# Ten of sixteen input tiles of the out-projection's second half as seven-product blocks, in the stream that later runs the up-projection

## The chip, the core and the metric

One core of one Trainium2 chip runs the whole program. The metric is the device time in microseconds (us) of one execution. The median of three executions of the kernel before is 2817.67 us (2817.4 to 2818.12); the profiled execution took 2819.0 us, of which its trace covers a span of 2816.9 us.

TensorE (PE) multiplies, VectorE (DVE), ScalarE (ACT) and GpSimd (POOL) do elementwise work, and SyncE (SP) issues most DMA transfers. Each engine works through its own instructions in order and waits on semaphores.

## The reference, cut to what matters

One layer of a hybrid decoder on 544 tokens (512 of a prompt, 32 of eight samples), all in fp32:

```python
proj = rmsnorm(x, norm_mix_w) @ w_in              # 2048 -> 9248 columns
y    = rmsnorm(ssd(...) * silu(z), ssd_norm_w)    # 2048 channels, "SSD half"
u    = cf_a * sigmoid(cf_g)                       # 2048 channels, "conv half"
u    = silu(layernorm(causal_dwconv(u, 31 taps)))
x    = x + concat([y, u]) @ w_out                 # out-projection, 4096 -> 2048
h    = rmsnorm(x, norm_ffn_w)
g, v = split(causal_dwconv(h @ w_up, 3 taps))     # 2048 -> 2 x 5504
x    = x + (silu(g) * v) @ w_down
out  = rmsnorm(x, norm_final_w)
```

The states of the three convolutions and of the SSD are outputs too.

## The kernel before

Channels stand on partitions in tiles of 128, and the 544 tokens stand in the free dimension as two halves of 272. A matrix product takes one 128x128 piece of weights and one half of the tokens. Each fp32 operand is split into a rounded part h and a remainder l (both fp32r), and three products are summed: h*xh, h*xl and l*xh. So a pair of weight tile and input tile costs 3 matmuls per half, 6 in all.

The work runs in two machines, one after the other.

**Jobs** (`job`, `run_jobs`, lines 137 to 219). A job makes one output tile of 128 channels from 16 input tiles in four blocks of four. `pump` keeps up to five weight blocks loaded (`raw`, 128x512) and three or four split (`wh` on ACT, line 118; `wl` on POOL or DVE, line 119). `tick` runs between blocks: it issues what `delay` and `store` put off, and one step of the generators in `bg`. Jobs in order: the first three columns of the input projection run together ("dt"), then the rest of it, then the out-projection's SSD half ("oy", 16 jobs, each times the norm factor `ry`, plus the residual `xT` on POOL, stored to DRAM as `xr_dram`), then its conv half ("ou", 16 jobs, evacuated by adding to the tile read back from `xr_dram`). While "oy" runs, `ln_gen` normalizes the 16 conv tiles `U` and splits each into `Uh` and `Ul`.

**Items** (lines 1194 to 1285, loop at 1558). One stream of products, prepared two items ahead: `prep_h` (ACT cast, line 1254), `prep_l` (DVE, line 1263), `product` on PE, `evac` of the item before. A `Group` of seven items computes two output tiles from K pairs of input tiles by Strassen's scheme: the 2x2 blocks are two output tiles by (first K, second K input tiles) by two token halves. Seven block products replace eight, at 3*K matmuls each. Its weights come in five tiles; two of those are sums of two pieces, which are made by a plain load from SP followed by an accumulating DMA from POOL (line 1231); one more sum is made on DVE (`sum_a`, `sum_b`). The inputs' sums `T` are made by `prep_pair` (lines 1128 to 1152). A `Plain` item computes one output tile from K input tiles, 6*K matmuls. The stream holds 43 groups with K = 8 (up-projection, `xs` times `w_up`) and then the down-projection, mixed of `Plain` items and groups with K = 6. Five weight buffers (`wr`) rotate; `issue` starts the next load when a split or sum has read one.

The `T` pairs for the up-projection are made in the evacuations of "ou", the last two around the switch from jobs to items. The norm factor `r2` is computed there too (`rsqrt_gen`, matmuls with `ones`, line 239).

At the start, `start_step` (line 307) makes `xh` on ACT and `xl` on DVE for four input tiles at a time, and `squares` (line 338) makes the squares for the first norm, two of four on ACT and two on DVE, and adds them up. `dt_gen` computes the SSD step sizes; PE needs its `dA_tok` in the matmul at line 422.

Of the kernel before, what the change touches and what calls it, by code (L numbers as in the profile page):

```python
# [14 lines left out]
NT = 544  # L15
NH = 272
# [7 lines left out]
NS0 = 4  # L24
# [6 lines left out]
def hymba_step_kernel(ctx: ExitStack, tc: tile.TileContext, a: dict):  # L31
# [236 lines left out]
    with tc.manual_schedule():  # L268
# [69 lines left out]
        def squares(n):  # L338
            def f():
                for k in range(4 * n, 4 * n + 4):  # L340
                    x = xraw.pop(k)
                    sq = slot("sq") if k > 1 else acc[k]
                    if k % 4 < 2:
                        S.activation(sq, x, AF.Square)
                    else:
                        V.tensor_tensor(sq, x, x, ALU.mult)
                    if k > 1:
                        e, i = (G, 0) if k % 4 == 0 else (V, 1)
                        e.tensor_tensor(acc[i], acc[i], sq, ALU.add)
            return f  # L350
# [23 lines left out]
        def dt_gen():  # L374
# [626 lines left out]

        xr_dram = [dram.tile([128, NT], F32, name=f"xrd{t}") for t in range(16)]
        xre = {}
        Uh, Ul = {}, {}

        def ln_gen():
# [34 lines left out]
            def fin(t):  # L1041
                u = U_t.pop(t)

                def f1():
                    Uh[t] = slot("Uh", dt=F32R, side=t < NS0)
                    S.copy(Uh[t], u)

                def f2():
                    Ul[t] = slot("Ul", dt=F32R, side=t < NS0)
                    V.tensor_tensor(Ul[t], u, Uh[t].bitcast(F32), ALU.subtract)  # L1050
                V.tensor_tensor(u, u, R["rs"], ALU.mult)
                S.activation(u, u, AF.Silu, scale=cfw[:, t, 32:33], bias=cfw[:, t, 33:34])
                delay(1, f1)
                delay(2, f2)
            for t in list(range(U_SPILL, 16)) + list(range(NS0, U_SPILL)) + list(range(NS0)):
                if t == 0:
                    Cur.side = swap("side0", "side1", bufs=2 * NS0, side="right")
                fin(t)
                yield
            yield  # L1060
            yield
# [4 lines left out]
        def load_x(t):  # L1066
            xre[t] = slot("xre")
            Y.dma_start(out=flat(xre[t]), in_=a["xT"][t])

        def oy_pre(t):  # L1070
            def f():
                if t == 0:
                    bg.append(ln_gen())
                    load_x(0)
                if t + 1 < 16:
                    load_x(t + 1)
            return f

        def oy_evac(t):
            def go(ps):  # L1080
# [5 lines left out]
                def s1():  # L1086
                    G.tensor_tensor(o, o, xre.pop(t), ALU.add)

                def s2():
                    store(xr_dram[t], flat(o))  # L1090
                return [s0, s1, s2]
            return go

        for t in range(16):
            job("oy", out_srcs(t, 0), lambda k: (Yh[k], Yl[k]), oy_evac(t), G, oy_pre(t))

        xres, xs, T_t = {}, {}, {}
        fst = dict(acc=None)
        xr2_dram = [dram.tile([128, NT], F32, name=f"xs{t}") for t in range(16)]
        OT = [t for k in range(8) for t in (k, k + 8)]  # L1100

        def load_xr(i):
            t = OT[i]
            xres[t] = slot("xres")
            Y.dma_start(out=flat(xres[t]), in_=xr_dram[t])

        def ou_pre(i):
            def f():
                if i == 0:
                    while not idle():  # L1110
                        tick()
                    load_xr(0)
                if i + 1 < 16:
                    load_xr(i + 1)
                else:
                    delay(0, up_open)
                    for j, f in enumerate(x_pair(6)):
                        delay(j // 2, f)
            return f
# [34 lines left out]
        def x_pair(k):  # L1154
            return prep_pair(T_t, k, lambda: xs[k], lambda: xs[k + 8])

        NPRE = 6

        def ou_evac(i):
            t = OT[i]  # L1160

            def go(ps):
                x = xres.pop(t)
                sq = slot("sq")

                def s0():
                    V.tensor_tensor(x, mv(ps), x, ALU.add)
                    xs[t] = slot("xs")
                    S.activation(xs[t], x, AF.Copy, scale=nw[:, NW_FFN, t:t + 1])
                    store(xr2_dram[t], flat(x))  # L1170

                def s1():
                    S.activation(sq, x, AF.Square)
                    if fst["acc"] is None:
                        fst["acc"] = sq
                    elif i < 15:
                        G.tensor_tensor(fst["acc"], fst["acc"], sq, ALU.add)
                    else:
                        spawn(rsqrt_gen([fst["acc"], sq], setr("r2")), 3)
                steps = [s0, s1] if i < 15 else [lambda: None, s0, s1]  # L1180
                if i % 2 and i // 2 < NPRE:
                    steps += x_pair(i // 2)
                return steps
            return go

        for i in range(16):
# [504 lines left out]
```

## Time and profile before

| | |
|---|---|
| median of three executions | 2817.67 us |
| profiled execution, its span | 2819.0 us, 2816.9 us |
| PE busy | 2780.4 us of the span |
| DVE, ACT, POOL busy | 2089.3, 1211.1, 905.1 us |
| "ou" jobs | 1198.0 to 1391.8 us of the span |
| up-projection | 1392.9 to 2313 us |
| down-projection and last norm | 2314 to 2817 us |

PE is busy almost all the time, and the idle time sits in a few places: the first 50 us, the switch from jobs to items, and the last norm. The other engines have room on average. The DMA share of a stretch is the mean busy share of the core's 16 DMA engines.

### The profile page before, as it was taken

The page shows a single profiled execution, that of the slowest core. Times are in us where ns is not written, and L with a number is a line of the kernel's source. Part 1 is how long each engine was busy: PE and PEld are TensorE (multiplying, and loading weights), DVE is VectorE, ACT ScalarE, POOL GpSimd, SP SyncE. Part 2 cuts the span into 40 slices and gives each one's busy share as a digit, 9 for nine tenths or more (in the row PEclk, how much of TensorE's full clock was granted, in tenths as well). Part 3 has the DMA queues.
Part 4 walks back from the last instruction along what each step waited for, and adds up shares of the span by engine and source line. Part 5 has one row for each costly group of instructions (what it writes and reads, how often), then busy time and mean ns, then how long its engine had stood idle before and what let it go on. Part 6 is the DMA issues. An engine that isn't in the chain of part 4 may idle for free.

```text
span 2816.9 us, 55473 instructions
## 1 busy us (share of the span) xinstructions
PE 2780.4 (99%) x22214; PEld 2753.4 (98%) x22214; DVE 2089.3 (74%) x3180; ACT 1211.1 (43%) x1793; POOL 905.1 (32%) x922
## 2 busy tenths in 40 slices
PE   7999999999999999999999999999999999999998
PEld 7999999999999999999999999999999999999997
DVE  7576665677777778344498888888888887778775
ACT  4555444333333324334344444444444444344344
POOL 4476668666676765511100000000000000100103
PEclk9999999999999999999999999999999999999999
DMA  4233343333332354444467777777777776765761
GB/s 166 82 116 115 95 144 103 124 108 104 101 101 92 97 161 126 138 133 133 146 177 195 191 186 195 190 185 193 194 185 191 194 200 193 179 185 154 174 186 64
DMA packets 194371, 422.29 MB, mean 150 GB/s; under 512 B 38080, under 2 KB 42816, under 8 KB 194112
## 3 DMA queue, kind: packets, MB, share of 16 engines
q1 hardware_dynamic: 177120, 361.07, 41.2%
q0 software_dynamic: 16992, 57.68, 11.6%
q8 instruction: 174, 2.85, 0.4%
q14 instruction: 85, 0.70, 0.1%
HBM read 376.25 MB, written 42.41 MB: 149 GB/s over the span
## 4 chain that ended last, share of the span: by engine, by line
PE 95%; DVE 3%; DMA 1%; issue 1%; ACT 0%; SPq 0%; DVEq 0%; POOLq 0%; ACTq 0%
PE mm L229 43%; PE st L1281 13%; PE st L1279 13%; PE st L1280 13%; PE st L229 6%; PE ax L229 2%; DMA x<-in_xT 1%; DVE o L501 1%; PE ax L660 1%; PE ax L599 0%; DVE sl L1263 0%; PE ax L664 0%; PE ax L629 0%; PE ax L757 0%; PE ax L763 0%
## 5 line engine op out<-in xcount | busy, mean ns | idle before, releaser
L1281 PE MATMUL st<-Th,sl 128*128 128x272 f32 x2640 | 762.7, 289 | 2.6 <-DVE sl L1263 2.6
L1279 PE MATMUL st<-Th,sh 128*128 128x272 f32 x2640 | 762.3, 289 | 1.4 <-ACT sh L1254 1.4
L1280 PE MATMUL st<-Tl,sh 128*128 128x272 f32 x2640 | 761.7, 289 | 0.0
L119 POOL TENSOR_TENSOR wl<-raw,wh 128x512 fp32r<-128x512 f32 x336 | 448.9, 1339 | 408.0 <-ACT wh L118 360.5
L1254 ACT CAST sh<-wr 128x1024 fp32r<-128x1024 f32 (+3 forms) x343 | 327.1, 954 | 416.8 <-PE st L1280 334.9
L1281 PEld LDWEIGHTS st<-Th,sl 128*128 128x128 f32 x2640 | 496.8, 188 | 3.9 <-DVE sl L1263 3.9
L1279 PEld LDWEIGHTS st<-Th,sh 128*128 128x128 f32 x2640 | 496.9, 188 | 1.7 <-ACT sh L1254 1.6
L1280 PEld LDWEIGHTS st<-Tl,sh 128*128 128x128 f32 x2640 | 496.8, 188 | 0.0
L229 PE MATMUL mm<-xh,wh 128*128 128x272 f32 x2304 | 483.4, 291 | 7.4 <-ACT xh L313 7.4
L229 PE MATMUL mm<-xl,wh 128*128 128x272 f32 x2304 | 479.4, 289 | 4.8 <-DVE xl L315 4.8
L118 ACT CAST wh<-raw 128x512 fp32r<-128x512 f32 x416 | 255.4, 616 | 525.3 <-PE mm L229 415.6
L229 PE MATMUL mm<-xh,wl 128*128 128x272 f32 x2304 | 478.5, 289 | 0.0
L1263 DVE TENSOR_TENSOR sl<-wr,sh 128x1024 fp32r<-128x1024 f32 (+3 forms) x343 | 377.9, 1102 | 58.7 <-ACT sh L1254 58.6
L229 PEld LDWEIGHTS mm<-xh,wh 128*128 128x128 f32 x2304 | 368.1, 188 | 16.3 <-ACT xh L313 7.4
L229 PEld LDWEIGHTS mm<-xl,wh 128*128 128x128 f32 x2304 | 365.4, 188 | 6.2 <-DVE xl L315 6.2
L229 PEld LDWEIGHTS mm<-xh,wl 128*128 128x128 f32 x2304 | 365.2, 188 | 0.0
L1231 POOL DMA_DIRECT2D wr<-in_w_up x86 | 74.9, 871 | 829.5 <-DVE ws L1245 235.4
L942 DVE SCALAR_TENSOR_TENSOR ax<-w,cfw,ax 128x512 f32<-128x512 f32 x448 | 302.5, 746 | 7.1 <-ACT ax L918 6.8
L1254 ACT CAST sh<-ws 128x1024 fp32r<-128x1024 f32 (+1 forms) x118 | 117.1, 992 | 264.1 <-DVE ws L1241 147.0
L1263 DVE TENSOR_TENSOR sl<-ws,sh 128x1024 fp32r<-128x1024 f32 (+1 forms) x118 | 136.0, 1153 | 30.6 <-ACT sh L1254 21.1
L1231 POOL DMA_DIRECT2D wr<-in_w_down x32 | 27.9, 871 | 368.6 <-DVE pd L1405 141.6
L119 DVE TENSOR_TENSOR wl<-raw,wh 128x512 fp32r<-128x512 f32 x80 | 70.2, 883 | 94.6 <-ACT wh L118 94.6
(317 smaller groups left out, 4979.0 us busy)
## 6 DMA issues: line engine op xcount, KB each, us to landing
wr<-in_w_up SPq DMA_DIRECT2D x215, 512.0 KB, 4.8
raw<-in_w_in SPq DMA_DIRECT2D x292, 256.0 KB, 3.2
wr<-in_w_up POOLq DMA_DIRECT2D x86, 512.0 KB, 8.0
wr<-in_w_down SPq DMA_DIRECT2D x96, 384.0 KB, 3.5
raw<-in_w_out SPq DMA_DIRECT2D x128, 256.0 KB, 3.0
wr<-in_w_down POOLq DMA_DIRECT2D x32, 384.0 KB, 5.5
ad<-ra SPq DMA_DIRECT2D x43, 272.0 KB, 7.9
ar<-ad SPq DMA_DIRECT2D x43, 272.0 KB, 4.0
```

The costliest lines, as they stand in the source:

```text
L118: S.copy(h[:, :n], r[:, :n])
L119: (cur["wl"] or eng).tensor_tensor(l[:, :n], r[:, :n], h[:, :n].bitcast(F32), ALU.subtract)
L229: T.matmul(o, lhsT=w[:, c], rhs=x[:, hf, :], start=first, stop=last)
L501: V.scalar_tensor_tensor(o[:, 0:568], w[:, i:i + 568], scw[:, t, i:i + 1], o[:, 0:568], ALU.mult, ALU.add)
L660: T.matmul(yps[ro:ro + 64, c4[c]], lhsT=xdt[c][:, q, :], rhs=MT[:, c4[c]], start=True, stop=c == 0)
L942: V.scalar_tensor_tensor(p, w[:, i:i + 512], wt(i), p, ALU.mult, ALU.add)
L1231: G.dma_start(out=t, in_=more, accum_op=ALU.add)
L1254: S.copy(h, src)
L1263: V.tensor_tensor(l, src, h.bitcast(F32), ALU.subtract)
L1279: T.matmul(outs[0], lhsT=h[:, c], rhs=xh_, start=k == 0, stop=False)
L1280: T.matmul(outs[0], lhsT=h[:, c], rhs=xl_, start=False, stop=False)
L1281: T.matmul(outs[0], lhsT=l[:, c], rhs=xh_, start=False, stop=k == o.K - 1)
```

## The change

Of the conv half's 16 input tiles, ten (tiles 6 to 15) become five pairs, whose products go through `Group`s with K = 5, one group for each pair of output tiles, eight groups. The other six tiles (0 to 5) go through 16 `Plain` items with K = 6. These 56 + 16 items stand at the head of the stream; the "ou" jobs are gone, and the stream's weight buffers open in the last "oy" job. `ln_gen` makes the sums `T_u` of the five pairs and stores the six other tiles to DRAM (`un_dram`), from where they are read back and split while the groups run. "oy" no longer adds the residual: it stores the scaled product alone. For each output tile the stream loads `xT` into `xres` and lets POOL add `xr_dram` by an accumulating DMA. `prep_pair` for the up-projection runs as tasks beside the `Plain` items, the last pair in the first up item. In the very first item the products with `l` come last. The evacuation of the groups (`block_evac`) is the one that the down-projection had. The squares at the start are all made on ACT. `dt_gen` gets one more `yield`.

```diff
@@ squares
-                    if k % 4 < 2:
-                        S.activation(sq, x, AF.Square)
-                    else:
-                        V.tensor_tensor(sq, x, x, ALU.mult)
+                    S.activation(sq, x, AF.Square)
@@ ln_gen, after the norm factor
+            for t in range(UP):
                 fin(t)
+                store(un_dram[t], flat(U_t.pop(t)))
                 yield
+            for i in range(NU):
+                p, q = UP + i, UP + NU + i
+                fin(p)
+                fin(q)
+                yield
+                f = prep_pair(T_u, i, lambda: U_t[p], lambda: U_t[q])
...
+        def load_xr(t):
+            xres[t] = slot("xres")
+            Y.dma_start(out=flat(xres[t]), in_=a["xT"][t])
+
+        def add_xr(t):
+            G.dma_start(out=flat(xres[t]), in_=xr_dram[t], accum_op=ALU.add)
...
@@ oy_pre, t == 15
+                    while not idle():
+                        tick()
+                    load_xr(0)
+                    load_xr(8)
+                    delay(0, up_open)
+                    delay(2, lambda: add_xr(0))
+                    delay(3, lambda: add_xr(8))
@@ oy_evac
-                def s1():
-                    G.tensor_tensor(o, o, xre.pop(t), ALU.add)
...
-        for i in range(16):
-            job("ou", out_srcs(OT[i], 1), lambda k: (Uh[k], Ul[k]), ou_evac(i), V, ou_pre(i))
@@ product
-                T.matmul(outs[0], lhsT=l[:, c], rhs=xh_, start=False, stop=k == o.K - 1)
+                if q:
+                    T.matmul(outs[0], lhsT=l[:, c], rhs=xh_, start=False, stop=k == o.K - 1)
+            for k in range(0 if q else o.K):
+                T.matmul(outs[0], lhsT=l[:, k * 128:k * 128 + 128], rhs=o.T[m, k][0], start=False, stop=k == o.K - 1)
@@ before the up-projection's groups
+        for i in range(8):
+            lo, hi = (wout[t, :, 2048 + UP * 128:4096] for t in (i, i + 8))
+            q = len(items)
+            Group(lo, hi, NU, T_u, block_evac(i))
+            if i:
+                at_item(q - 5, lambda i=i: load_xr(i))
+                at_item(q - 2, lambda i=i: add_xr(i))
+                at_item(q - 2, lambda i=i: load_xr(i + 8))
+                at_item(q + 1, lambda i=i: add_xr(i + 8))
+        for t in range(UP):
+            at_item(28 + 4 * t, lambda t=t: u_load(t))
+            at_item(30 + 4 * t, lambda t=t: u_split(t))
...
+        for i in range(16):
+            Plain(wout[OT[i], :, 2048:2048 + UP * 128], UP, lambda k: (Uh[k], Ul[k]), out_evac(i))
+        for k in range(8):
+            st = prep_pair(T_t, k, lambda k=k: xs[k], lambda k=k: xs[k + 8])
+            for f, d in zip(st, (2, 2, 3, 3)):
+                at_item(q + 2 * k + d, f)
```

How the instructions move, in the built programs. First the start, DVE, kernel before (`xl` is a remainder of the input, `sq` a square, `acc` a sum of squares):

```order
L315 SCALAR_TENSOR_TENSOR xl_242<-x_88,nw,xh_240 128x544
L346 TENSOR_TENSOR sq_281<-x_86 128x544
L349 TENSOR_TENSOR acc_148<-acc_148,sq_281 128x544
L346 TENSOR_TENSOR sq_284<-x_88 128x544
L349 TENSOR_TENSOR acc_148<-acc_148,sq_284 128x544
L315 SCALAR_TENSOR_TENSOR xl_317<-x_96,nw,xh_315 128x544
```

The same place on DVE, changed kernel:

```order
L315 SCALAR_TENSOR_TENSOR xl_248<-x_88,nw,xh_246 128x544
L346 TENSOR_TENSOR acc_148<-acc_148,sq_287 128x544
L346 TENSOR_TENSOR acc_148<-acc_148,sq_290 128x544
L315 SCALAR_TENSOR_TENSOR xl_323<-x_96,nw,xh_321 128x544
L315 SCALAR_TENSOR_TENSOR xl_327<-x_98,nw,xh_325 128x544
```

The two squares left DVE's order between two sets of remainders; on ACT they now stand ahead of the next weight block's cast and the next four `xh`. The same happens in each of the four sets.

Second SP's queue in the conv half. Kernel before, one "ou" job and the start of the next (`raw` weight blocks, `xs` a stored result, `xres` a tile read back):

```order
L102 DMA raw_14896<-in_w_out 128x512
L102 DMA raw_14928<-in_w_out 128x512
L102 DMA raw_14961<-in_w_out 128x512
L102 DMA raw_14995<-in_w_out 128x512
L180 DMA xs_173<-xres_14635 128x544
L1105 DMA xres_15044<-xrd_151 128x544
```

Changed kernel, SP, a group's seven loads (`wr` weight tiles):

```order
L1180 DMA wr_14856<-in_w_out 128x640
L1073 DMA xres_14879<-in_xT 128x544
L1180 DMA wr_14883<-in_w_out 128x640
L1180 DMA wr_14886<-in_w_out 128x640
L1180 DMA wr_14932<-in_w_out 128x640
L1073 DMA xres_14955<-in_xT 128x544
L1180 DMA wr_14982<-in_w_out 128x640
```

Five weight tiles and two residual tiles stand in SP's queue for a group of seven items, where one read, one store and four blocks stood for a job.

Third POOL's queue in the conv half. Kernel before, from the last "oy" job on:

```order
L119 TENSOR_TENSOR wl_14511<-raw_14475,wh_14510 128x512
L1087 TENSOR_TENSOR oy_14505<-oy_14505,xre_14253 128x544
L1087 TENSOR_TENSOR oy_14630<-oy_14630,xre_14380 128x544
L1177 TENSOR_TENSOR sq_14759<-sq_14759,sq_14888 128x544
L1177 TENSOR_TENSOR sq_14759<-sq_14759,sq_15039 128x544
```

Changed kernel, POOL, a group's four accumulating transfers and the next group's first:

```order
L1182 DMA wr_14856<-in_w_out 128x640
L1182 DMA wr_14886<-in_w_out 128x640
L1076 DMA xres_14879<-xrd_157 128x544
L1076 DMA xres_14955<-xrd_165 128x544
L1182 DMA wr_15028<-in_w_out 128x640
```

POOL's sums of squares moved out to the `Plain` items, and in their place stand four accumulating DMAs a group, in one order: two on weight tiles, two on residual tiles.

## Rows read from the trace of the kernel before

**Rows 1.** The page, part 1: busy us (share), instructions of an engine.
```profile
PE 2780.4 (99%) x22214; PEld 2753.4 (98%) x22214; DVE 2089.3 (74%) x3180; ACT 1211.1 (43%) x1793; POOL 905.1 (32%) x922
```
**Rows 2.** Stretches: length, busy us (records) by engine, PE clock, DMA share, GB/s.
```profile
40.00:50.00 10.00, 6.69 (x30) 5.20 (x29) 6.81 (x10) 1.41 (x3) 1.94 (x2) 0.83 0.08 28
1198.00:1391.80 193.80, 193.80 (x1538) 193.75 (x1536) 89.63 (x133) 70.30 (x119) 22.71 (x17) 1.00 0.44 136
1391.80:1431.00 39.20, 34.29 (x230) 32.49 (x229) 30.42 (x40) 17.19 (x22) 1.74 (x2) 0.91 0.61 155
1431.00:2314.20 883.20, 882.42 (x7003) 881.98 (x7003) 768.59 (x1130) 425.79 (x549) 71.32 (x82) 1.00 0.73 190
```
**Rows 3.** PE's waits from 0 to 1001 us: total, times, longest.
```profile
PE mm L229 <- DVE xl L315: 4.8, 6, 2.8
PE ax L239 <- DVE acc L349: 2.2, 1, 2.2
PE ax L422 <- DVE dA_tok L417: 1.1, 1, 1.1
```
**Rows 4.** PE in order of time, jobs to items: start, us, instruction, [idle before].
```profile
1392.90 0.39 PE L1279 MATMUL st<-Ta,sh 128*128 128x272 f32 x1 [0.93 <-ACT sh L1254]
...
1394.16 0.40 PE L1281 MATMUL st<-Ta,sl 128*128 128x272 f32 x1 [0.74 <-DVE sl L1263]
...
1394.84 0.43 PE L1279 MATMUL st<-Ta,sh 128*128 128x272 f32 x1
1395.07 0.43 PE L1280 MATMUL st<-Ta,sh 128*128 128x272 f32 x1
...
1423.29 0.29 PE L1279 MATMUL st<-Ta,sh 128*128 128x272 f32 x1
...
1445.74 0.29 PE L1279 MATMUL st<-Ta,sh 128*128 128x272 f32 x1
...
1466.90 0.29 PE L1279 MATMUL st<-Ta,sh 128*128 128x272 f32 x1
```
**Rows 5.** PE, first matmuls of two successive groups with K = 6.
```profile
2404.60 0.29 PE L1279 MATMUL st<-Ta,sh 128*128 128x272 f32 x1
...
2420.49 0.29 PE L1279 MATMUL st<-Ta,sh 128*128 128x272 f32 x1
```
**Rows 6.** The squares at the start: DVE's (ns min/median/max), then ACT's (busy, mean ns).
```profile
L346 DVE TENSOR_TENSOR sq<-x x8: 710/1526/1818, 10.4 to 44.5; 128x544 f32<-128x544 f32 x8
...
L344 ACT ACTIVATE sq<-x 128x544 f32<-128x544 f32 x6 | 3.6, 650 | 0.0
```
**Rows 7.** DMA queues, 1440 to 2300 us (K = 8): packets, MB, share.
```profile
q1 hardware_dynamic: 47075, 120.01, 45.2%
q0 software_dynamic: 11802, 42.97, 27.7%
```
**Rows 8.** DMA queues, 2388 to 2500 us (K = 6).
```profile
q1 hardware_dynamic: 5040, 13.76, 40.8%
q0 software_dynamic: 1990, 5.45, 30.2%
```
**Rows 9.** A stretch of 10 us with both DMA queues busy.
```profile
1500.00:1510.00 10.00, 10.00 (x82) 10.00 (x81) 8.68 (x15) 3.34 (x4) 0.88 (x1) 1.00 0.97 239
```
**Rows 10.** The page, part 6: issues, KB, median us to landing.
```profile
wr<-in_w_up SPq DMA_DIRECT2D x215, 512.0 KB, 4.8
...
wr<-in_w_up POOLq DMA_DIRECT2D x86, 512.0 KB, 8.0
wr<-in_w_down SPq DMA_DIRECT2D x96, 384.0 KB, 3.5
...
wr<-in_w_down POOLq DMA_DIRECT2D x32, 384.0 KB, 5.5
```
**Rows 11.** DVE's groups by form, 2314.2 to 2752.2 us.
```profile
L1388 DVE TENSOR_TENSOR xres<-st,xres 128x272 f32<-128x272 f32 x94 | 36.9, 434 | 16.8 <-PE st L229 16.8
...
L1263 DVE TENSOR_TENSOR sl<-wr,sh 128x640 fp32r<-128x640 f32 x16 | 13.1, 817 | 0.0
```

More of the change, by code (lines that the diff above doesn't have):

```diff
@@ L23 @@
 U_SPILL = 8
-NS0 = 4
+NU = 5
 NSTART = 12
@@ L999, in hymba_step_kernel @@
                 zq += 1
+        UP = 16 - 2 * NU
+        T_u = {}
+        un_dram = [dram.tile([128, NT], F32, name=f"un{t}") for t in range(UP)]
         xr_dram = [dram.tile([128, NT], F32, name=f"xrd{t}") for t in range(16)]
-        xre = {}
-        Uh, Ul = {}, {}
         def ln_gen():
@@ L1086, in s1 @@
                 def s1():
-                    G.tensor_tensor(o, o, xre.pop(t), ALU.add)
-                def s2():
                     store(xr_dram[t], flat(o))
-                return [s0, s1, s2]
+                return [s0, s1]
             return go
[L1094 to L1119, printed above, removed]
         def split_into(h, l, src):
@@ L1152, in prep_pair @@
             return first, lambda: pair(q(), (1, 5)), second, third
[L1154 to L1170, printed above, removed]
-                def s1():
[L1173 to L1184, printed above, removed]
-        for i in range(16):
-            job("ou", out_srcs(OT[i], 1), lambda k: (Uh[k], Ul[k]), ou_evac(i), V, ou_pre(i))
+        for t in range(16):
+            job("oy", out_srcs(t, 0), lambda k: (Yh[k], Yl[k]), oy_evac(t), G, oy_pre(t))
         KW = 8 * 128
@@ new lines, in hymba_step_kernel, with f_load @@
+        q = len(items)
+        for i in range(16):
[4 more added lines that the diff above has]
+                at_item(q + 2 * k + d, f)
+            at_item(q + 2 * k + 3, lambda k=k: (xs.pop(k), xs.pop(k + 8)))
+        fstate, fcw = [], None
+        def f_load():
+            nonlocal fcw
+            fcw = cload("fcw", [128, 86, 4])
+            for i in range(3):
+                n = min(29, 86 - 29 * i)
+                fstate.append(slot("fs", [128, 29, 16]))
+                Y.dma_start(out=fstate[i][:, 0:n, :], in_=a["ffn_state"][:, 29 * i:29 * i + n, :])
@@ L1287, in hymba_step_kernel @@
+        at_item(q + 4, f_load)
+        QU = len(items)
         cg = {}
@@ L1544, in hymba_step_kernel @@
         pst = swap("pst", "pmm", bufs=4, space=bass.MemoryType.PSUM)
-        x7 = x_pair(7)
         prep_h(0)
         prep_l(0)
-        while len(later) > 1:
-            run_later()
-        x7[0]()
         prep_h(1)
-        fcw = cload("fcw", [128, 86, 4])
-        fstate = []
-        for i in range(3):
-            n = min(29, 86 - 29 * i)
-            fstate.append(slot("fs", [128, 29, 16]))
-            Y.dma_start(out=fstate[i][:, 0:n, :], in_=a["ffn_state"][:, 29 * i:29 * i + n, :])
+        drain_later()
         for q in range(len(items)):
```

125 lines of the change are left out of this document (69 added, 56 removed).

## The prediction

> **What bounds the kernel now.** I read four views: the page's busy times, the table by stretch, PE's waits, and PE in order of time where the table shows idle PE. PE is busy for 2780.4 of 2816.9 us [rows 1], so a term counts only if it takes work off PE or closes one of its gaps. The table places the gaps [rows 2]: the "ou" stretch is full (193.80 of 193.8 us), the up-projection nearly so (882.42 of 883.2), but from 1391.8 to 1431 PE has 34.29 of 39.2 us and a granted clock of 0.91. At the start PE waits 4.8 us for `xl`, 2.2 us for the squares' sum and 1.1 us for `dA_tok` [rows 3]. At the switch from jobs to items it waits 0.93 us for the first cast and 0.74 us for the first remainder, after which its matmuls stand 0.23 us apart instead of 0.126 [rows 4]: the lower of the clock's two levels, 1.2 instead of 2.4 GHz, after these two waits.
>
> **Term A, PE's work.** "ou" has 16 jobs of 16 input tiles at 6 matmuls, 1536, in 193.8 us: 126.2 ns each [rows 2]. The change issues 8 groups x 7 items x 5 pairs x 3 = 840 and 16 items x 6 tiles x 6 = 576, together 1416. A group with K = 6 shows the same pace for block products: 15.89 us for 126 matmuls, 126.1 ns [rows 5]. So 120 matmuls x 126.1 ns = 15.1 us go, all from PE's full stretch. This is counting; I give it 0.3 us either way.
>
> **Term B, the switch.** The first up group takes 1423.29 - 1392.90 = 30.39 us, the second 22.45, the steady third 21.16 [rows 4]. The excess is 9.23 + 1.29, and 1.1 us pass between the last "ou" matmul and the first item (1391.8 to 1392.90): 11.6 us. In that time DVE and ACT still prepare the last up pairs. In the changed kernel the switch comes after "oy", when `T_u` is ready, its first weights have 0.625 of the columns, and the first remainder is wanted only after ten matmuls. I leave there 0.8 us for the first cast and 1.8 us for one spell at the lower clock. The four matmuls with `ones` for `r2` move to the new border of the conv half and the up-projection and stay: about 1.8 us. The last up pair is made inside the first up item, behind the evacuation of the last `Plain` item, and I leave 1.5 us for that wait. Together 6 instead of 11.6: -5.5 us. Bounds: -9 if only the cast and `r2` remain, 0 if each of the two borders costs half of what the one did.
>
> **Term C, the start.** Eight squares leave DVE; one takes between 710 and 1818 ns there [rows 6]. DVE is what PE waits for at this time, for 4.8 + 2.2 us [rows 3]; the extra `yield` gives `dA_tok` one block more, for 1.1 us. The clock's mean of 0.83 from 40 to 50 us [rows 2] follows the wait for the sum; with the wait goes perhaps 0.7 us of it. At most 8.8 us are to be had. Against it ACT does 8 x 650 ns = 5.2 us more [rows 6], two squares ahead of every next cast and set of `xh`. Part of each `xl` then waits for ACT in place of DVE, so I take three quarters: -6.5 us. Bounds: -9, and +1 if ACT becomes late for a set by the two squares (1.3 us) and nothing else is won.
>
> The Trainium skill, page "SBUF — State Buffer", section "Who interferes with whom", says that a DVE instruction with two SBUF inputs is shut out while a GpSimd instruction that reads SBUF holds the shared pair, and that ScalarE never waits for it. The spread of 710 to 1818 ns for one instruction [rows 6] agrees. By the rule the squares on ACT cost 650 ns whatever POOL does, and all 8.8 us come back; by the row of PE's waits alone, some of them do. This changes nothing in the sum.
>
> **Term D, transfers in the block stretch.** This is the loss. A group with K = 5 is 105 matmuls, 13.24 us on PE, against 21.16 for an up group. In that time the DMA engines must bring five weight tiles (128 x 640 x 4 B = 0.328 MB), two of them again as accumulating transfers, two tiles of `xT` (0.2785 MB) and two accumulating tiles of `xr_dram`: 2.20 MB on SP's queue and 1.21 MB on POOL's. "oy" had `xT` under long jobs; here it is beside products that are shorter than before.
>
> Prices from the stream: in the up stretch SP's queue took 45.2% of 860 us for 120.01 MB, 3.24 us per MB of all 16 engines, and POOL's 27.7% for 42.97 MB, 5.54 [rows 7]. With K = 6 they are 3.32 and 6.2 [rows 8]. A group thus needs 2.20 x 3.24 + 1.21 x 5.54 = 13.8 us by the first and 14.8 by the second, where PE needs 13.24. I take 14.3. The table's 0.73 for the up stretch [rows 2] is the scale: there 21.16 us of PE stand against 15.4 of transfers.
>
> Groups 1 to 7 must be brought while the stream runs: 7 x 14.3 = 100.1 us, and five of the six tiles of `un_dram` fall into the same time, 5 x 0.2785 x 3.24 = 4.5. The best 10 us of both queues hold 0.97 [rows 9]; over a whole stretch I allow 0.94. So (100.1 + 4.5)/0.94 = 111.3 us. The last weights are wanted at item 53 of 56, at 53 x 1.89 = 100.2 us. Missing: 11 us. PE can run on for two prepared items, 3.8 us, which leaves 7. Waits may bring the lower clock again, as at the switch; for that 3 us. D = +10 us. Bounds: 0 with 13.8 us at full use (101 us against 100.2 + 3.8); +20 if the chain of the accumulated tiles sets the pace instead: load 3.5 us and accumulation 5.5 [rows 10], one residual accumulation ahead of it on POOL's queue, by its size 3.9 (an estimate), and three tile-wide instructions for sum and splits, 2.5 [rows 11]: 15.4, so 8 x 2.2 = 17 and some clock.
>
> DVE hides behind this: nine tile-wide instructions x 0.82, seven of half width x 0.434, two full ones under 0.82 [rows 11] are at most 12.0 us of 13.24. The pairs `T_u` replace the splits of `U` under "oy", where PE waits for nobody. In the `Plain` items one tile of 0.39 MB in 4.5 us leaves the transfers idle half of the time. Both cost nothing as long as "oy" keeps three blocks split ahead; if it does not, a few us are lost there.
>
> **Sum.** -15.1 - 5.5 - 6.5 + 10 = -17.1 us, against the profiled execution's 2819.0: 2801.9. The median is 1.3 us lower than that execution, so 2800.6 us.
>
> **Rivals.**
> - *The transfers fit* (D = 0 to 3): the K = 6 groups run at 15.89 us [rows 5] with 71% of the DMA engines' time [rows 8], and packet times may hold some waiting that a fuller queue would use. Against it: 0.97 is the most that both queues reach together. Time 2800.6 - 9 = 2791.6. The Trainium skill, page "DMA: Bandwidth & Descriptors", section "Anatomy of one DMA — SWDGE (gpsimd) path", fits 2.0 us plus bytes at 436 GB/s; by that a group's 3.41 MB would need 7.8 us, this rival. The measured shares [rows 7, 8] do not agree: they come to 13.8 and more.
> - *The accumulations set the pace* (D = 20): 2810.6. For it: POOL's landings of 5.5 to 8.0 us [rows 10], in order, each behind its own load.
> - *The start gains nothing* (C = +1): ACT is then the late one. 2808.
> - *Slower*: the same POOL chain at the landing times of the up stretch, 4.8 + 8.0 us [rows 10], a residual accumulation by its size 4.2, and the 2.5: 19.5 us a group. The terms A to C are 27.1 us; eight groups must lose 32.7 to end 5.6 us slower, so this decides from a period of 17.3 us on. At 19.5 they lose 8 x 6.3 = 50, and the time is 2840. Against it: those landings are of tiles 1.6 times as large.
>
> **Chances.** Forecast 0.48, transfers fit 0.20, accumulations 0.16, no gain at the start 0.10, slower 0.06. The measurement tells 0.2% (5.6 us) from no change; that is 2812.0. Of the accumulation case half lies below it, of the start case 0.07. Faster 0.48 + 0.20 + 0.08 + 0.07 = 0.83, same 0.11, slower 0.06. The range runs from B and C at their best with D = 0 to 3 (about 2789) to D = 20 with a poorer start (2816).
>
> **What would show it.** A: 1416 matmuls in the conv half. B: the first up group close to 24 us, and no double gap at the first item. C: PE's waits for `xl` and the sum under 2 us, none for `dA_tok`. D: the first three groups near 13.3 us, later ones 14 to 16, a DMA share above 0.9 in that stretch, and PE waiting for casts and sums whose releaser is a DMA. I am wrong if the groups stay at 13.3 us throughout, if they pass 17 us, or if "oy" itself becomes longer.

## The result: slower by 1%, and the profile after

The changed kernel takes 2845.89 us (median of 4 runs, 2838.24 to 2849.51) against 2817.89 for the kernel before on the same chip: ratio 1.0095, 95% interval 1.0082 to 1.0107. It is 28 us slower; 2800.6 was predicted. Its profiled execution took 2846.8 us, 27.8 more than the one of before.

The page, part 1, of the changed kernel, against [rows 1]:

```profile
PE 2779.6 (98%) x22094; PEld 2749.9 (97%) x22094; DVE 2161.8 (76%) x3314; ACT 1234.5 (43%) x1827; POOL 906.8 (32%) x938
```

PE has 120 instructions less, as counted, and is busy for as long as before: where its clock is lower, a matmul is busy for longer (0.59 us for the first one after the wait at 1427.9 us, 0.29 for those before it). The stretches tell more (length, then busy us of PE, PEld, DVE, ACT and POOL with records, PE clock, DMA share, GB/s), against [rows 2]:

```profile
40.00:50.00 10.00, 8.32 (x60) 7.88 (x60) 7.71 (x8) 3.43 (x6) 3.21 (x3) 1.00 0.17 59
...
1192.00:1205.30 13.30, 13.30 (x105) 13.30 (x106) 11.81 (x20) 5.71 (x9) 2.10 (x3) 1.00 0.66 178
1205.30:1324.85 119.55, 101.72 (x738) 99.40 (x737) 79.83 (x131) 39.81 (x62) 22.45 (x26) 0.93 0.87 213
1324.85:1417.70 92.85, 81.33 (x578) 79.42 (x577) 64.95 (x101) 44.20 (x71) 19.44 (x15) 0.93 0.46 128
1417.70:1450.90 33.20, 25.81 (x179) 25.08 (x178) 24.95 (x32) 14.88 (x20) 3.11 (x3) 0.85 0.52 149
1450.90:2333.00 882.10, 881.36 (x6996) 880.92 (x6995) 768.46 (x1131) 423.42 (x545) 71.37 (x82) 1.00 0.73 190
```

The start has gained. The first group of the block stretch runs at PE's pace (13.3 us); the other seven take 119.55 us where 7 x 13.24 = 92.7 would do. The `Plain` stretch takes 92.85 us where 576 x 0.1261 = 72.6 would do, though its transfers are idle half of the time and no engine is full. The first up group takes 33.2 us, the steady one 21.16. From the second up group to the end the two kernels take 1394.2 and 1393.6 us: there nothing has changed.

Four kinds of wait of PE stand in these places (total, times, longest):

```profile
PE st L1233 <- DVE sl L1214: 17.6, 10, 5.0
PE st L229 <- DVE xres L1300: 11.5, 6, 2.8
PE st L1230 <- ACT Ta L1106: 7.4, 1, 7.4
PE st L1230 <- ACT sh L1205: 1.6, 2, 1.0
```

PE waits for DVE's weight remainders, then for PSUM banks that DVE has not emptied, then for the last up pair; the fourth row, two waits for a weight cast, is small. What DVE itself waits for in the block stretch (1191 to 1325 us):

```profile
DVE xres L1253 <- DMA xres<-xrd: 17.1, 4, 6.0
DVE oy L1097 <- PE mm L229: 11.5, 1, 11.5
DVE Ul L1107 <- ACT Uh L1106: 11.0, 5, 5.5
DVE sl L1214 <- ACT sh L1205: 7.0, 13, 0.8
```

The second row is the end of "oy" and costs nothing. The first is `block_evac` at a residual tile whose accumulation has not landed, the third `u_split` at a reloaded tile of U whose cast, and whose load, are late. DVE's queue holds the next weight remainders behind both.

### The profile page after: what moved, and what is told of

It reads as the page before. It is cut to its first block, busy times and chain, and to the rows that moved or that the text cites. A ratio compares the mean times of both kernels' runs of the same rounds, so it can differ in the third digit from the quotient of the medians.

```text
span 2845.1 us, 55518 instructions
## 1 busy us (share of the span) xinstructions
PE 2779.6 (98%) x22094; PEld 2749.9 (97%) x22094; DVE 2161.8 (76%) x3314; ACT 1234.5 (43%) x1827; POOL 906.8 (32%) x938
## 5 line engine op out<-in xcount | busy, mean ns | idle before, releaser
L1233 PE MATMUL st<-Th,sl 128*128 128x272 f32 x2880 | 835.9, 290 | 18.4 <-DVE sl L1214 18.4
L1230 PE MATMUL st<-Th,sh 128*128 128x272 f32 x2880 | 834.6, 290 | 1.0 <-ACT sh L1205 1.0
L1231 PE MATMUL st<-Tl,sh 128*128 128x272 f32 x2880 | 833.8, 290 | 0.0
L1233 PEld LDWEIGHTS st<-Th,sl 128*128 128x128 f32 x2880 | 545.0, 189 | 21.2 <-DVE sl L1214 21.2
L1230 PEld LDWEIGHTS st<-Th,sh 128*128 128x128 f32 x2880 | 545.3, 189 | 1.4 <-ACT sh L1205 1.4
L1231 PEld LDWEIGHTS st<-Tl,sh 128*128 128x128 f32 x2880 | 545.0, 189 | 0.0
L1214 DVE TENSOR_TENSOR sl<-wr,sh 128x1024 fp32r<-128x1024 f32 (+3 forms) x399 | 427.4, 1071 | 56.0 <-ACT sh L1205 55.9
L1182 POOL DMA_DIRECT2D wr<-in_w_up x86 | 74.9, 871 | 836.0 <-DVE pu L1348 390.7
L1205 ACT CAST sh<-ws 128x1024 fp32r<-128x1024 f32 (+2 forms) x134 | 128.7, 961 | 314.3 <-DVE ws L1192 162.2
L1214 DVE TENSOR_TENSOR sl<-ws,sh 128x1024 fp32r<-128x1024 f32 (+2 forms) x134 | 149.2, 1114 | 36.2 <-ACT sh L1205 26.6
L1230 PE MATMUL st<-Ta,sh 128*128 128x272 f32 x480 | 138.7, 289 | 8.0 <-ACT Ta L1106 7.4
L1182 POOL DMA_DIRECT2D wr<-in_w_down x32 | 27.8, 869 | 368.9 <-DVE pd L1256 129.2
```

What stands on the lines that cost most here:

```text
L1182: G.dma_start(out=t, in_=more, accum_op=ALU.add)
L1205: S.copy(h, src)
L1214: V.tensor_tensor(l, src, h.bitcast(F32), ALU.subtract)
L1230: T.matmul(outs[0], lhsT=h[:, c], rhs=xh_, start=k == 0, stop=False)
L1231: T.matmul(outs[0], lhsT=h[:, c], rhs=xl_, start=False, stop=False)
L1233: T.matmul(outs[0], lhsT=l[:, c], rhs=xh_, start=False, stop=k == o.K - 1)
```

## The experiments

The lengths in the table are of one profiled execution each. Block is the time from the first group's first matmul to the first `Plain` item's, Plain from there to the first up group, Up 1 that group; the last two columns are the median and its ratio to the kernel before in the same call (95% interval).

| | Block | Plain | Up 1 | us | ratio |
|---|---|---|---|---|---|
| PE's pace | 105.9 | 72.6 | 21.16 | | |
| changed kernel | 132.8 | 92.9 | 33.1 | 2845.9 | 1.0095 (1.0082 to 1.0107) |
| e1 start alone | | | | 2811.8 | 0.9975 (0.9966 to 0.9985) |
| e2 residual in oy | 115.1 | 93.6 | 32.7 | 2837.0 | 1.0065 (1.0050 to 1.0080) |
| e3 residual early | 129.8 | 93.3 | 32.9 | 2840.7 | 1.0074 (1.0058 to 1.0091) |
| e4 no square sum | 128.0 | 79.8 | 32.6 | 2831.9 | 1.0044 (1.0029 to 1.0059) |
| e5 residual on DVE | 117.8 | 92.3 | 34.2 | 2833.9 | 1.0056 (1.0043 to 1.0070) |
| e6 order of pairs | 132.4 | 75.5 | 32.4 | 2826.6 | 1.0028 (1.0017 to 1.0039) |
| e7 squares on PE | 133.2 | 85.5 | 31.6 | 2837.6 | 1.0066 (1.0050 to 1.0081) |
| e8 all mended | 110.2 | 79.3 | 22.2 | 2805.3 | 0.9956 (0.9943 to 0.9968) |
| e9 residual, no queue | 131.0 | 92.6 | 32.7 | 2843.6 | 1.0092 (1.0073 to 1.0110) |
| e10 POOL's sum again | 109.3 | 74.9 | 29.0 | 2804.7 | 0.9956 (0.9944 to 0.9969) |
| e11 residual in DRAM | 109.5 | 75.3 | 29.0 | 2807.1 | 0.9964 (0.9950 to 0.9977) |
| e12 border as in e8 | 109.3 | 75.3 | 29.1 | 2803.9 | 0.9949 (0.9935 to 0.9962) |
| e13 U apart | 123.8 | 92.3 | 32.7 | 2839.6 | 1.0074 (1.0051 to 1.0097) |
| e14 U and residual early | 121.2 | 93.1 | 33.3 | 2833.0 | 1.0056 (1.0033 to 1.0079) |

Edits outside a stretch move its length by some us (Block is 128.0 and 133.2 in e4 and e7, where nothing of it was touched), so differences under 5 us there are not read.

**e1: the start.** On the kernel before:

```diff
-                    if k % 4 < 2:
-                        S.activation(sq, x, AF.Square)
-                    else:
-                        V.tensor_tensor(sq, x, x, ALU.mult)
+                    S.activation(sq, x, AF.Square)
+            yield          # ahead of the first use of dA_tok
```

> The kernel before with the start edits alone (all squares of the first norm on ACT, one more yield ahead of the first use of dA_tok). Start theory: the changed kernel's last oy matmul came 6.8 us earlier than before (1191.2 against 1198.0), and nothing behind it can take that back, since every later stretch is bound by PE: 2817.9 - 6.8 = 2811.1 us, with PE's wait for xl near 1.4 us instead of 4.8. Rival: part of the 6.8 us comes from the oy stretch of the changed kernel, which no longer loads xT nor adds it on POOL; then this kernel gains only 3 to 5 us and ends near 2814.

Measured: 2811.75 us against 2818.61, 6.9 less. PE's waits from 0 to 1001 us are now, against [rows 3]:

```profile
PE mm L229 <- DVE xl L315: 1.9, 4, 0.8
PE ax L239 <- DVE acc L346: 1.7, 1, 1.7
```

PE's wait for `dA_tok` is gone. The gain is the start's own, and it stays to the end. The two edits were not run apart.

**e2, e5: the residual out of the block stretch.**

```diff
 def load_xr(t):
-    Y.dma_start(out=flat(xres[t]), in_=a["xT"][t])
+    Y.dma_start(out=flat(xres[t]), in_=xr_dram[t])
-def add_xr(t): ...
 # oy_evac, with xT loaded into xre by oy_pre
+    G.tensor_tensor(o, o, xre.pop(t), ALU.add)     # e2; e5: V
     store(xr_dram[t], flat(o))
```

> The changed kernel, but xT is loaded and added by POOL under oy as in the kernel before, and the block stretch loads the finished sum with one plain load a tile: 16 loads of xT and 16 accumulating transfers less in that stretch. Late-residual theory (DVE, in order, stands 17.1 us at the addition into a residual tile whose accumulation has not landed, and the remainders for the next products stand behind it): these waits go, the block stretch falls from 132.9 to 112 to 116 us, the whole to about 2828. Rival, the reloads of U (DVE stands 11.0 us for the cast of a reloaded U tile, ACT 7.2 us for its load): the stretch stays above 125. Rival, accumulation of the weights on POOL's queue: also above 125, with PE waiting for sums and casts whose releaser is a weight DMA.

> The kernel of e2 with one word changed: under oy the addition of xT is made by DVE instead of POOL. In e2 the block stretch fell to 115.1 us, but oy's last matmul came at 1197.3 us instead of 1191.1, with PE waiting for POOL's weight remainders (wl) after 1155 us. POOL theory: POOL is late there because the addition stands ahead of the remainders on its queue while DVE makes the pairs of U; on DVE the addition costs nothing, oy ends near 1191.5, the whole is 2837 - 6 = 2831 us. Rival, slots: the tiles for xT take the slots that the pairs need, and oy ends near 1197 as in e2 wherever the addition is made.

The block stretch of e2:

```profile
1198.20:1313.30 115.10, 109.87 (x841) 106.66 (x842) 92.52 (x151) 45.69 (x71) 14.02 (x15) 1.00 0.78 210
```

and what DVE waits for there:

```profile
DVE sl L1221 <- ACT sh L1212: 8.2, 16, 0.8
DVE Ul L1114 <- ACT Uh L1113: 8.1, 6, 2.2
DVE ws L1199 <- DMA wr<-in_w_out: 4.3, 3, 2.6
```

17.7 us went, and the wait for the residual with them. But "oy" ended at 1197.3 us, 6.2 later, so the whole gained 11.3 us by the profiled executions and 8.9 by the medians. PE's longest kind of wait in "oy", in e2:

```profile
PE mm L229 <- POOL wl L119: 3.0, 5, 0.7
```

and in e5:

```profile
PE mm L229 <- POOL wl L119: 2.0, 4, 0.6
```

With the addition on DVE "oy" ends at 1193.8. So POOL's addition was 3.5 of the 6.2 us; the rest is not its doing, and in e5 PE still waits for `wl`. e2 takes away two things at once, late waits and accumulating transfers; the next runs keep the transfers.

**e3, e9: the same transfers, earlier.**

```diff
-at_item(q - 5, load_xr(i));  at_item(q - 2, add_xr(i))
-at_item(q - 2, load_xr(i + 8));  at_item(q + 1, add_xr(i + 8))
+at_item(q - 12, load_xr(i));  at_item(q - 9, add_xr(i))           # e3
+at_item(q - 9, load_xr(i + 8));  at_item(q - 6, add_xr(i + 8))
+at_item(q - 19, load_xr(i));  at_item(q - 17, load_xr(i + 8))     # e9, adds as in e3
```

What would stand ahead of item 0 in the first groups is issued at items 0 to 3.

> The changed kernel with the same transfers of the residual, each issued seven items (one group, about 13 us) earlier. Late-residual theory: the bytes are the same but nothing waits for them, so the stretch falls to 112 to 118 us as without them. Throughput rival (the transfer engines cannot bring a group in 13.24 us): an earlier issue only moves the queue, the stretch stays at 125 to 133 us and DVE waits for weights instead.

> The changed kernel with all transfers of the residual kept, accumulations issued seven items earlier as in e3, and the loads of xT that they wait for issued ten to twelve items ahead of them. In e3 the block stretch stayed at 129.8 us, but POOL's queue stood 24.2 us for loads of xT, with the weights' accumulations behind. Queue theory (an accumulation that waits for its load holds up the weights): the wait for xT goes and the stretch falls below 120 us. Throughput theory (8 groups at 14.3 us of transfers, never more than about 0.9 in use): the wait goes too, the stretch stays at 126 us or more, with a transfer share of 0.88 to 0.95.

DVE's two longest kinds of wait in the block stretch of e3:

```profile
DVE Ul L1107 <- ACT Uh L1106: 15.7, 6, 5.8
DVE ws L1192 <- DMA wr<-in_w_out: 12.7, 4, 4.3
```

the same of e9:

```profile
DVE Ul L1107 <- ACT Uh L1106: 13.7, 6, 5.4
DVE ws L1192 <- DMA wr<-in_w_out: 11.6, 4, 4.0
```

and e9's block stretch:

```profile
1191.70:1322.70 131.00, 116.12 (x841) 113.61 (x842) 92.25 (x152) 45.56 (x71) 24.58 (x28) 0.92 0.85 213
```

The wait for the residual is gone in both, POOL's wait for xT fell from 24.2 us in e3 to 9.9 in e9, and the stretch stayed at 130 us: DVE now waits for U and for weights. The late residual was therefore not the whole cause, against what I held after e2. Nor were the transfers full over the whole stretch: the share was 0.85, under what the throughput theory had asked for in e9. But the edit has a price of its own. In e9 the eight groups take 13.37, 19.67, 14.36, 14.30, 21.18, 14.20, 20.71 and 13.21 us, in the changed kernel 13.36, 13.26, 15.55, 18.39, 19.73, 15.94, 21.20 and 15.42. The second group is 6.4 us longer, with transfers of later groups now issued ahead of it or in it (in e4, e6, e7 and e13, which leave the residual alone, it takes 13.53 to 15.88); the third, fourth, sixth and eighth are 9.2 us shorter in sum; the two groups above 20 us hold DVE's longest waits for U (4.4 and 5.4 us). That left two candidates: too many bytes, or U.

**e13, e14: the U reloads.** e13 is the changed kernel with this edit alone, e14 has e9's as well.

```diff
 def u_split(t):
-    Uh[t], Ul[t] = slot(...), slot(...)
-    split_into(Uh[t], Ul[t], ur.pop(t))
+    Uh[t] = slot(...);  S.copy(Uh[t], ur[t])
+def u_low(t):
+    Ul[t] = slot(...);  V.tensor_tensor(Ul[t], ur.pop(t), Uh[t], ALU.subtract)
-at_item(28 + 4 * t, u_load(t));  at_item(30 + 4 * t, u_split(t))
+at_item(25 + 4 * t, u_load(t));  at_item(30 + 4 * t, u_split(t));  at_item(31 + 4 * t, u_low(t))
```

> The changed kernel with the edit of the U reloads alone: loads three items earlier, and DVE's remainder one item behind ACT's cast. Throughput theory (the bytes of the residual's accumulations are what the stretch cannot carry): DVE's 11.0 us of waits for the cast of U go over to other late transfers, the block stretch stays at 127 to 133 us. Late-landing theory (each landing that DVE's queue waits for, in order, costs PE directly, since DVE has only some 1 us a group to spare): 7 to 10 us go, the stretch falls to 122 to 126 us.

> e13 and e9 together: the same bytes as in the changed kernel, with the residual's transfers and the U loads all early and nothing of them waited for in order. Late-landing theory: both waits gone, the stretch falls to 110 to 116 us, as in e2 and e8, at a transfer share of 0.95 or more. Throughput theory: the stretch stays at 124 us or more, the share under 0.9, and DVE and ACT wait for weight tiles in place of U and residual.

e13: DVE's wait for U is gone, 9.0 us of the stretch with it (6.3 by the medians), as the late-landing theory said; its wait for the residual stays at 15.4 us. In e14 both waits are gone and the stretch is 121.2 us, 11.6 less than the changed kernel's (12.9 by the medians), and no shorter. 70 us of the changed kernel's block stretch:

```profile
1210.00:1280.00 70.00, 61.09 (x447) 59.83 (x445) 45.90 (x76) 21.95 (x35) 14.06 (x16) 0.93 0.89 215
```

the same 70 us of e14:

```profile
1210.00:1280.00 70.00, 61.91 (x448) 59.94 (x449) 51.22 (x84) 25.02 (x40) 16.05 (x19) 0.95 0.98 242
```

and DVE's longest kind of wait in e14:

```profile
DVE ws L1192 <- DMA wr<-in_w_out: 18.0, 6, 4.4
```

With no wait left for U or the residual the DMA engines are full (0.98), and DVE waits for weights. The groups take 13.36, 19.18, 14.55, 14.30, 15.05, 17.45, 13.25 and 14.09 us. The second is as long as in e9, and full of transfers (0.99):

```profile
1205.45:1224.63 19.18, 15.30 (x108) 14.86 (x106) 12.03 (x19) 5.66 (x9) 4.98 (x7) 0.91 0.99 256
```

The e14 result lies between the two theories, and each was right for a part. Of the 26.9 us over PE's pace, 9.0 go when the U reloads are early (e13), 2.6 more when the residual is early too (e14, less than can be read), and 15.3 stay. e8 and e10 to e12 below have U early and of the residual only one plain load a tile in this stretch, and they still stand 3.4 to 4.3 us over PE's pace; so some 11 to 12 of the 15.3 us come with the residual's transfers. e2, without the accumulating ones, ran at a share of 0.78.

How a full queue reaches PE is shown by DVE's wait for weights. In the trace each of the six in e14 ends with the landing of an accumulated weight tile, which the sum of two weight tiles needs; one of them, as POOL issues the transfer and as DVE's sum follows it:

```profile
1236.04 0.86 POOL L1182 DMA_DIRECT2D wr<-in_w_out  x1 [7.58 <-DVE xres L1259]
1241.61 0.82 DVE L1192 TENSOR_TENSOR ws<-wr,wr 128x640 f32<-128x640 f32 x1 [2.20 <-DMA wr<-in_w_out]
```

So load, accumulation and sum form a chain, 5.6 us of it for this accumulation. Whether the bytes alone or this chain sets the 14.3 to 15.05 us of three groups in a row is not told apart by any run.

**e4, e7: the squares' sum.**

```diff
 # out_evac, e4
-elif i < 15:
-    G.tensor_tensor(fst["acc"], fst["acc"], sq, ALU.add)
 # e7, three items later
+    T.matmul(ps[hf], lhsT=ones_r, rhs=sq[:, hf, :], start=i == 0, stop=i == 15)
```

> The changed kernel without POOL's 14 additions that sum the squares for the second norm (the sum is left out, only the first and the last square are used; everything else is computed). In the Plain stretch DVE's remainders of 544 columns took 1152 ns against 720 elsewhere and those of 272 took 1448 against 441. Port theory (POOL's additions slow DVE's two-input instructions): these means fall to 720 to 730 and 440, 12 us of DVE time go, and the Plain stretch falls from 92.9 to about 80 us. Rival, the chain of ACT and DVE behind one another in the making of the pairs: the means fall but the stretch stays near 90 us.

> The changed kernel with the second norm's squares summed by PE: two single-pass matmuls of a ones tile with each squares tile, as it comes, in place of POOL's additions and of the four last ones matmuls. e4 left the sum out and the Plain stretch fell from 92.9 to 79.8 us. Port theory: the same here, 79.8 + 32 x 0.13 = 84 us, less some 1.8 us at the border, the whole about 2846 - 14 + 4 - 2 = 2834. Rival: PE waits for the squares (ACT), its order ties it to ACT's lateness; then the stretch stays near 90 us.

DVE's instructions by form in the `Plain` stretch of the changed kernel (count, busy us, mean ns, idle before):

```profile
L1107 DVE TENSOR_TENSOR Tl<-tr,Th 128x544 fp32r<-128x544 f32 x12 | 13.8, 1152 | 11.0 <-ACT Th L1106 11.0
L1300 DVE TENSOR_TENSOR xres<-st,xres 128x272 f32<-128x272 f32 x30 | 11.7, 429 | 4.9 <-PE st L229 4.9
L1107 DVE TENSOR_TENSOR Ta<-xs,Ta 128x272 fp32r<-128x272 f32 x7 | 10.1, 1448 | 11.8 <-ACT Ta L1106 11.8
```

The same of e4:

```profile
L1300 DVE TENSOR_TENSOR xres<-st,xres 128x272 f32<-128x272 f32 x30 | 11.7, 433 | 4.9 <-PE st L229 4.9
L1107 DVE TENSOR_TENSOR Tl<-tr,Th 128x544 fp32r<-128x544 f32 x12 | 8.7, 726 | 10.7 <-ACT Th L1106 10.7
L1107 DVE TENSOR_TENSOR Ta<-xs,Ta 128x272 fp32r<-128x272 f32 x7 | 3.1, 443 | 11.8 <-ACT Ta L1106 11.8
```

e4 leaves the sum of the squares out. Without POOL's additions these remainders take 726 and 443 ns instead of 1152 and 1448, and the stretch 13 us less, as the port theory said; the `xres` row, which takes one operand from PSUM, is the same in both. The Trainium skill, page "SBUF — State Buffer", section "Who interferes with whom", shuts out a DVE instruction with two SBUF inputs while GpSimd reads SBUF; the three rows agree. DVE's idle time behind ACT (11.0 and 11.8 us) is unchanged. In e7 PE's 32 matmuls more leave 85.5 us, near the 84 expected.

**e6: the order of a pair.**

```diff
-for f, d in zip(prep_pair(...), (2, 2, 3, 3)): at_item(q + 2 * k + d, f)
+at_item(q + 2 * k + 1, a)     # ACT: cast for Ta
+at_item(q + 2 * k + 2, b)     # DVE: Ta's remainder, r, s; ACT: three casts
+at_item(q + 2 * k + 3, c)     # DVE: three remainders
 # and in the items: prep_l(q + 2) ahead of the tasks
```

> The changed kernel with the making of the pairs T_t in the Plain items in another order: casts one step ahead of the remainders that need them, and the pair's instructions on DVE behind the next weight remainder; POOL's sum of squares stays. Order theory (DVE and ACT wait for each other inside a pair, 13.7 + 12.1 us of DVE, and at the border the last Plain evacuation stands behind the previous pair, 7.4 us of PE's wait): the Plain stretch falls from 92.9 to about 85 us (the 12 us by which POOL slows DVE remain), the first up group from 33.1 to 27 us, the whole from 2845.9 to about 2832. Rival, DVE's work alone sets the pace: 8.3 us a pair by the unslowed durations and some 10 with POOL's interference, of 9.1 us on PE; the Plain stretch stays at 90 to 93 us and only the border gains, whole about 2840.

The `Plain` stretch of e6:

```profile
1324.00:1399.50 75.50, 73.67 (x579) 73.09 (x577) 65.32 (x102) 44.15 (x71) 20.42 (x15) 1.00 0.55 157
```

DVE's remainders in it:

```profile
L1340 DVE TENSOR_TENSOR Tl<-tr,Th 128x544 fp32r<-128x544 f32 x12 | 15.9, 1365 | 0.0
```

PE's waits from there to 1440 us:

```profile
PE st L1231 <- DVE Ta L1325: 6.3, 1, 6.3
PE st L229 <- DVE xres L1300: 1.8, 2, 1.3
```

17.4 us went although POOL still slows DVE (1365 ns): better than either theory. In the making of the pairs DVE no longer stands behind ACT (0.0; 4.5 us are left ahead of weight remainders). POOL's price and the ping-pong were one chain; either cure shortens it, and they don't add: e8 below has both, and without the 4.0 us of its added matmuls it is at 75.3 us, as e6 is. The border did not gain: 6.3 us of wait in place of 7.4.

**e8, e10, e12, e11: together.** e8 has the edits of e5, e6, e7 and e13. e10 gives the sum of the squares of tiles 0 to 12 back to POOL and puts the first up item's weights behind the last pair; e12 is e10 without that last edit; e11 is e10 with the residual made in DRAM under "oy":

```diff
 # e10, e12: three squares and POOL's sum at the end through fp32r matmuls with ones
+spawn(rsqrt_gen([fst["acc"], fst[13], fst[14], sq], setr("r2"), ones_r), 3)
 # e11
+Y.dma_start(out=xr_dram[t], in_=a["xT"][t])
+G.dma_start(out=xr_dram[t], in_=flat(o), accum_op=ALU.add)
```

> The changed kernel with the edits of e5, e6 and e7 together, and the casts and remainders of the reloaded U tiles one item apart with the loads three items earlier. If the losses are those found (late residual 17.7 us of the block stretch, POOL against DVE 12 us less 4 of PE, border 6 us, U reloads some us) and do not hide one another: block stretch 110 us, Plain 78, first up group 26, the whole 2845.9 - 22 - 13 - 7 = about 2804 us. Rival: DVE is nearly full in both stretches (about 12.2 of 13.24 us a group and 8.3 of 9.1 us a pair), each small wait still shows, block stretch 115 and Plain 82: about 2814.

> e8, but the squares of tiles 0 to 12 are summed by POOL again and only three tiles and that sum go through single-pass ones matmuls, and in the first up item the sum of weights stands behind the last pair. In e6 the order alone brought the Plain stretch to 75.5 us with POOL's sums in it, in e8 it was 79.3 with 32 matmuls more. Order theory: Plain 75.5 us, first up group 22 to 24 us, the whole e8's 2805.3 - 4 = 2801. Port rival: POOL slows DVE, DVE falls behind at the border as in e6 (6.6 us wait): the first up group 28 to 30 us, the whole 2805 or more.

> e10, but the residual is made in DRAM under oy: xT is copied to the residual's buffer, and the scaled oy tile is added to it by an accumulating transfer, so that no tile of xT takes a slot and DVE makes no addition. In e5 and e8 oy's last matmul came at 1193.8 and 1194.2 us against 1191.1 in the changed kernel. Slot theory: oy ends at 1191.2, the whole 3 us under e10, about 2798. Rival: those transfers take the weights' time under oy, or oy's loss is DVE's pairs; oy ends at 1194 or later, the whole as e10.

> e10 with the first up item in e8's order again (the weights' sum and the cast of item 2 ahead of the last pair). In e10 the Plain stretch was 74.9 us and the first up group 28.98 us, with PE waiting 2.3 us for that cast and 1.5 us for the last pair and the lower clock behind them; in e8 79.3 and 22.15. Order theory: the moved cast was e10's fault, the group comes to 23 to 25 us, the whole to 2804.7 - 5 = 2800. Port rival: POOL's sums leave DVE with more work at the end of the Plain items (63.9 us in e10 against 55.6 in e8) and the backlog is paid at the border in either order; the group is 27 us or more and the whole stays at 2804 to 2807.

The `Plain` stretch of e8:

```profile
1305.30:1384.60 79.30, 76.71 (x606) 76.49 (x605) 55.62 (x106) 48.45 (x76) 1.73 (x2) 1.00 0.52 149
```

and of e12:

```profile
1304.60:1379.90 75.30, 73.71 (x578) 73.14 (x577) 64.20 (x101) 45.29 (x73) 18.86 (x14) 1.00 0.55 157
```

PE's wait in the first up group of e12:

```profile
1387.17 0.59 PE L1238 MATMUL st<-Ta,sh 128*128 128x272 f32 x1 [4.31 <-DVE Ta L1342]
```

and that group's length and clock:

```profile
1379.90:1409.00 29.10, 24.79 (x178) 24.58 (x177) 23.50 (x30) 14.06 (x19) 1.78 (x2) 0.88 0.62 171
```

e8 fell as expected (2805.3 us for 2804), and its first up group is within 1.0 us of PE's pace. POOL's sum saves 4 us in the `Plain` stretch and pays 7 at the border, in either order (29.0 and 29.1): DVE is busy for 8.6 us more in the stretch (64.20 against 55.62), and PE waits for it behind the border. e8's stretch also holds one wait of PE for the cast of `ones`, 2.6 us, which an earlier cast could save; no run tried that. The port rival held, and the order theory failed in e10 and in e12. e11's "oy" ended at 1193.6 us: the slots were not the reason for its loss, which stays unexplained (PE waits 1.4 us for `wl`). The four cannot be told apart by their times; all are faster than both kernels, e12 by 0.5% against before.

## Why the prediction was wrong, point by point

| term | predicted | measured | from |
|---|---|---|---|
| A, 120 matmuls less | -15.1 | -15.1 | counts, pace of 13.3 us in the first group |
| B, the switch | -5.5 | +2.6 | 0.9 + 12.0 + 1.3 for 11.6 |
| C, the start | -6.5 | -6.8 | e1 alone: -6.9 |
| D, block stretch | +10 | +26.9 | 132.8 - 105.9 |
| `Plain` items | 0 | +20.3 | 92.9 - 72.6 |
| sum | -17.1 | +27.9 | profiled executions: +27.8 |

- **A and C** were right, by size and place; in C the 0.83 clock from 40 to 50 us went to 1.00, as supposed. That C's size came out so well is in part luck: its three quarters were a choice, and the rows of PE's waits account for 4.5 of e1's 6.9 us (4.8 to 1.9, 2.2 to 1.7, 1.1 to none).
- **`Plain` items: this step failed outright.** "In the `Plain` items one tile of 0.39 MB in 4.5 us leaves the transfers idle half of the time. Both cost nothing" looked at the transfers alone (0.46, as said). It did not count that the making of eight up pairs, which had stood under 193.8 us of "ou", was moved to 72.6 us. DVE had 89.63 us of work in "ou" [rows 2] and has 64.95 here, 89% of PE's 72.6 us and part of it slowed by POOL. So the 22.8 us that it waited for ACT in its order had no room, and PE waited 11.5 us for PSUM banks. e6 removes 17.4 of the 20.3 us by order alone.
- **D** was mis-sized, and part of it is a step that failed. The part of the full transfers, forecast at 10, is 15.3 at most (e14), and 11 to 12 if the 3.4 to 4.3 us that e8 and e10 to e12 keep are taken off. Another 11.6, 9.0 of them with the U reloads, came through the sentence "DVE hides behind this ... 12.0 us of 13.24": the busy time was right (92.52 us over e2's eight groups, 11.6 each), but some 1.6 us of room a group does not hold a wait of 5.5 us for a U tile or of 6.0 us for a residual. The first two groups were as predicted (13.36 and 13.26 us), the third was not (15.55 for 13.3), and of the later ones three passed 17 us, which the prediction had named as a sign of being wrong. Nor was the share above 0.9: it was 0.87 over the seven groups, since part of the time the transfers waited for buffers that a late DVE had not freed. POOL's queue, in the changed kernel's block stretch, waited for plain loads of weights to land and for such buffers:

```profile
POOL wr L1182 <- DMA wr<-in_w_out: 31.5, 4, 11.2
POOL wr L1182 <- DVE sl L1214: 27.1, 5, 7.5
```

- **B**: the first border was as good as said (0.9 us, no double gap). At the second I left "1.5 us for that wait"; it was 7.4, and the group's clock was 0.85. DVE's order of time at the border (start, us, instruction, [idle before]):

```profile
1420.99 0.43 DVE L1133 SCALAR_TENSOR_TENSOR tr<-tr,xs 128x272 f32<-128x272 f32 x1
1422.24 0.73 DVE L1107 TENSOR_TENSOR Tl<-tr,Th 128x544 fp32r<-128x544 f32 x1 [0.82 <-issue]
1422.88 1.22 DVE L1214 TENSOR_TENSOR sl<-wr,sh 128x1024 fp32r<-128x1024 f32 x1
1424.02 1.22 DVE L1192 TENSOR_TENSOR ws<-wr,wr 128x1024 f32<-128x1024 f32 x1
1425.15 0.78 DVE L1300 TENSOR_TENSOR xres<-st,xres 128x272 f32<-128x272 f32 x2
1427.91 0.44 DVE L1107 TENSOR_TENSOR Ta<-xs,Ta 128x272 fp32r<-128x272 f32 x1 [1.97 <-ACT Ta L1106]
```

  The evacuation of the last `Plain` item (`xres`, 1425.15) stands behind the previous pair's work, a weight remainder and a sum of weights, though PE had finished that item at 1417.7. e4 without POOL's additions and e6 with another order both left this wait at 6 to 7 us; e8, with e6's order and no additions on POOL, has none.
- **The rivals.** The slower one came true in its sign, though only three of the eight groups passed its limit of 17.3 us and the `Plain` items did the rest. Its mechanism, POOL's chain of accumulations as the period of every group, is not what the changed kernel shows: of the three long groups two (18.39 and 19.73 us) hold a wait of DVE for an accumulated residual (5.2 and 6.0 us) and the longest (21.20) one for a cast of U (5.5 us). Accumulations that land late have a part in it, and in e14 they are what DVE waits for, so the chain is not excluded there. Its size for a residual accumulation, 4.2 us by its bytes, was short; measured, from issue to landing:

```profile
xres<-xrd POOLq DMA_DIRECT2D x14, 272.0 KB, 7.4
```

What stays open: e2 and e8 run 4 to 9 us over PE's pace in the block stretch, and e8's "oy" ends 3 us later than the changed kernel's; no run separates these. Nor was the accumulation of the weights, which e2's expectation names as a rival, ever taken away by itself.

## What to carry to other kernels

When work moves to a shorter stretch, divide each engine's busy time by the new length, for every engine and not for the transfers alone; one that comes out near 90% (DVE here: 92.5 of 105.9 us, 64.95 of 72.6) has little room left, and the waits inside its own order are then paid by PE. In such a stretch the order within a queue (a cast one step ahead of its remainder) can be worth more than the arithmetic that was saved: here 17 us against 15. An evacuation ahead of the next stage's preparation, which the border asks for, was not tried. A transfer that fits on average still costs if an in-order engine stands at its landing.

## What the runs showed of the hardware that was not expected

- Accumulating transfers cost the DMA engines 6.0 us per MB (in e14, from 1192 to 1318 us, 40.4% of 126 us for 8.52 MB), plain ones 3.1 (49.2% for 20.19 MB), against 5.54 to 6.2 and 3.24 to 3.32 in the stream [rows 7, 8]. So the price of accumulating did not fall with a fuller queue, that of plain transfers by some 5%; over 70 us the share reached 0.98, where I had allowed 0.94.
- Beside POOL's additions of 544 columns (mean 1402 ns) a DVE remainder of 272 columns took 1448 ns in place of e4's 443: a short instruction can lose twice its own length.
